# A two-layer MoE decoder trunk: f32r row broadcasts, low parts on VectorE, residual sum formed late, aligned ring of 38 weight pieces

## The chip, the cores and the metric

The kernel runs on one core of a Trainium2 chip. The metric is the device time of one execution in microseconds (us), as the median of several runs. A profile of one execution lies beside the runs.

## The reference

A sequence of 256 tokens of width 1024 goes through two layers. Each layer is a mixer (layer 0: a chunkwise mLSTM; layer 1: MoBA block-sparse attention) and a mixture of 16 experts (MoE). All is float32. Cut to what the change touches:

```python
shift, scale, gate = mods[layer, 0]          # from silu(c) @ w_ada + b_ada
y = mixer(modulate(x, shift, scale))
x = layer_norm(ALPHA * x + gate * y, ln_g[layer, 0], ln_b[layer, 0])
shift, scale, gate = mods[layer, 1]
h = modulate(x, shift, scale)
probs = softmax(h @ w_router)                # 16 experts in 4 groups
# best group by the sum of its top two (probs + b_router), then its top two experts
y = sum over the 2 experts of weight * (silu(h @ w_gate[e]) * (h @ w_up[e])) @ w_down[e]
x = layer_norm(ALPHA * x + gate * y, ln_g[layer, 1], ln_b[layer, 1])
```

The expert weights are 100.7 MB per layer and are all read, whatever the routing.

## The kernel before

**Weights.** All weights come in pieces of 512 KB (128 partitions x 1024 floats) that SyncE's queue (SP) issues in the order of the program. A piece goes into a slot of a ring and the slot is free when TensorE (PE) has used it. The ring has 20 slots (`RING * 2`), and around a MoE up to 17 more (`RING2`), so that 37 pieces can stand ready. By the addresses that the allocator gives in the built program, the 20 slots begin at multiples of 256 bytes within a partition and the 17 others 64 or 224 bytes past one.

**A MoE** uses 192 pieces: 8 blocks of two experts, each with a gate part, an up part and a down part of 8 pieces. The first block needs the routing; until then only prefetching can go on, and it stops when the ring is full.

**Routing chain, per layer.** The last mixer product `y(1,1)` on PE; VectorE (DVE) adds it to `xt` (L542, L543); PE transposes (`th`), ScalarE (ACT) copies to `xT`, PE forms `pr` and `pl`; DVE makes the logits `lg` (L993), ACT the exponentials `pexp`; DVE then walks through some 25 small operations (`s`, `ss` L1026, `pairs` L1036 to L1038, `el`, `gl`, `gn`, `en`) to `mask` (L1051). PE sums the mask into positions (`pp`), DVE makes `onehot` (L1075), PE gathers the chosen tokens into banks `ga` with products of `onehot` and the two float32r parts `xh` and `xl` of x, ACT and DVE modulate them into `xe` (L518, L520), and PE starts on the gate part (`pg`). All these wait for each other.

**Beside that chain.** `xl = x - xh` is made on GpSimd (POOL, L1003) in four pieces of 128x512. The residual sum `acc = ALPHA * (x * g + b)` is made on DVE in eight steps (L1295, L1296), from rows `lnps` that PE broadcasts from `rw` to all partitions (L497, sixteen float32 128x128 products per layer, each of which the trace records twice). The gate rows `adag` are broadcast the same way (L449, four float32 128x256 products per call, two calls per layer). In the MoE, `slots_T` transposes the one-hot matrix and sums the weights of the slots (`oT`, `wsl`, L1106 to L1118).

The order on each engine is that of a scheduler in the program which places instructions by their costs and what they wait for; `issue_after` holds one back until another is placed.

Of the kernel before, what the change touches and what calls it, by code (L numbers as in the profile page):

```python
# [18 lines left out]
P = 128  # L19
D = 1024  # L20
# [14 lines left out]
RING2 = 17  # L35
# [23 lines left out]
BIG = 1e30  # L59

def _columns(groups):

    at, span, o = {}, [], 0
    for g, names in enumerate(groups):
        o0 = o
        for n, w in names:
# [8 lines left out]
                             (("cb", KI), ("gn", KI), ("skip", KI), ("cw", 4 * KI), ("wif", KI * 8), ("bif", 2))))  # L75
CS, CS_SPAN, NCS = _columns(((("ident", P), ("sel4", 1), ("iota", SLOTS), ("selr", E)),
# [3 lines left out]
def constants():  # L80
# [16 lines left out]
    put("sel4", p % 32 == 0)  # L97
    m = np.zeros((P, 12))
# [50 lines left out]
def _body(ctx, tc, x, w_ada, a_w_in, a_wq, a_wk, a_wv, a_w_out, b_w_kv, b_wq, b_wo, moe_w_gate, moe_w_up,  # L149
# [6 lines left out]
    small = ctx.enter_context(tc.tile_pool(name="small", bufs=2))  # L156
    ring = ctx.enter_context(tc.tile_pool(name="ring", bufs=RING * 2))
# [13 lines left out]
    G.memset(rw, 0.0)  # L171
    nc.sync.dma_start(pk[0][:, 0:KD], pc[:, 0:KD])
# [158 lines left out]
    def ada_sum(j, hf, red, accs):  # L331

        ps = bankB(f"adaps{j}_{hf}")
        for z in range(2):
# [3 lines left out]
            if is_gate(j):  # L338
                for y in range(2):
                    r = 64 + 8 * (j // 3) + 4 * hf + 2 * z + y  # L340
                    T.matmul(o[:, P * y:P * y + P], ident[:, r:r + 32], rw, start=False, stop=(y == 1))
# [243 lines left out]
    wif = pe.tile([P, KI, 32], F32, name="wif")  # L585
    G.memset(wif, 0.0)
# [954 lines left out]
```

## Time and profile before

| | |
|---|---|
| median of 3 runs | 941.38 us (940.91 to 943.47) |
| the profiled execution's own time | 941.74 us |
| its span, first to last instruction | 940.0 us |
| mean granted TensorE clock | 0.986 of 2.4 GHz |
| PE busy | 905.2 us (96%) |
| DVE busy | 525.4 us (56%) |
| ACT, POOL busy | 336.0 us, 38.1 us |
| DMA | 318.56 MB, mean 339 GB/s |

The span has these stages: mixer A to about 310 us, routing of layer 0 to 332, MoE 0 to about 546, mixer B to 692, routing of layer 1 to 715, MoE 1 to about 922, and a tail to 940. A busy PE need not be the limit, since in a MoE its matmuls wait for pieces; the share of the DMA engines and the GB/s tell that apart.

### The profile page before, as it was taken

The page shows a single profiled execution, that of the slowest core. Times are in us where ns is not written, and L with a number is a line of the kernel's source. Part 1 is how long each engine was busy: PE and PEld are TensorE (multiplying, and loading weights), DVE is VectorE, ACT ScalarE, POOL GpSimd, SP SyncE. Part 2 cuts the span into 40 slices and gives each one's busy share as a digit, 9 for nine tenths or more (in the row PEclk, how much of TensorE's full clock was granted, in tenths as well). Part 3 has the DMA queues.
Part 4 walks back from the last instruction along what each step waited for, and adds up shares of the span by engine and source line. Part 5 has one row for each costly group of instructions (what it writes and reads, how often), then busy time and mean ns, then how long its engine had stood idle before and what let it go on. Part 6 is the DMA issues. An engine that isn't in the chain of part 4 may idle for free. (4 is left out here: it accounts for less than half of the span.)

```text
span 940.0 us, 14244 instructions
## 1 busy us (share of the span) xinstructions
PE 905.2 (96%) x5397; PEld 564.9 (60%) x5400; DVE 525.4 (56%) x992; ACT 336.0 (36%) x558; POOL 38.1 (4%) x48
## 2 busy tenths in 40 slices
PE   9999999999999899999999988999998999999995
PEld 5877988876777644334343478886764343434343
DVE  2476876867878823332333499898883223334317
ACT  3476666466564311111111054566542111101120
POOL 0010000000000200000000004021110000000000
PEclk9999999999999999999999998999998999999998
DMA  9999784787987979999999998877984999999992
GB/s 333 393 405 376 260 282 156 270 330 250 333 305 257 355 271 407 406 406 407 407 406 407 397 403 336 300 255 242 372 317 166 408 405 407 407 406 407 407 398 103
DMA packets 174253, 318.56 MB, mean 339 GB/s; under 512 B 10112, under 2 KB 28256, under 8 KB 174176
## 3 DMA queue, kind: packets, MB, share of 16 engines
q1 hardware_dynamic: 174032, 317.36, 91.2%
q8 instruction: 45, 0.74, 0.3%
q14 instruction: 32, 0.26, 0.1%
q10 hardware_dynamic: 144, 0.20, 0.1%
HBM read 316.47 MB, written 1.05 MB: 338 GB/s over the span
## 5 line engine op out<-in xcount | busy, mean ns | idle before, releaser
L1202 DVE SCALAR_TENSOR_TENSOR yl<-py,wsl,yh 128x512 fp32r<-128x512 f32 x28 | 21.0, 750 | 172.6 <-ACT yh L1201 172.6
L126 PE MATMUL pg<-w,xe 128*64 128x512 f32 x512 | 116.1, 596 | 0.0
L126 PE MATMUL pu<-w,xe 128*64 128x512 f32 x512 | 116.0, 596 | 0.0
L126 PE MATMUL py<-w,aT 128*64 128x512 f32 (+1 forms) x576 | 115.8, 547 | 0.2 <-DMA w<-in_moe_w_down_dram 0.2
L384 DVE SCALAR_TENSOR_TENSOR adacc<-ada,pk,adacc 128x512 f32<-128x512 f32 x112 | 87.3, 785 | 1.0
L126 PEld LDWEIGHTS py<-w,aT 128*64 128x64 f32 x576 | 40.9, 137 | 70.8 <-issue 61.2
L126 PEld LDWEIGHTS pu<-w,xe 128*64 128x64 f32 x512 | 35.7, 137 | 63.7 <-issue 61.4
L126 PEld LDWEIGHTS pg<-w,xe 128*64 128x64 f32 x512 | 34.8, 137 | 64.0 <-issue 58.9
L1168 ACT COPY aT<-aT 128x512 f32<-128x512 f32 x16 | 9.4, 585 | 141.0 <-PE aT L126 141.0
L542 DVE TENSOR_TENSOR lntmpe<-po,gate 128x512 f32<-128x512 f32 x56 | 36.1, 685 | 38.1 <-PE po L126 38.1
L1201 ACT ACTIVATE yh<-py,wsl 128x512 fp32r<-128x512 f32 x28 | 19.2, 687 | 81.1 <-PE py L126 81.1
L520 ACT ACTIVATE xe<-ga,coef 128x256 f32<-128x256 f32 x32 | 16.3, 561 | 76.6 <-PE ga L126 76.6
L262 PE MATMUL z<-hh,wz 128*128 128x256 f32 x128 | 37.6, 294 | 0.0
L543 DVE TENSOR_TENSOR acc<-acc,lntmpe 128x512 f32<-128x512 f32 x56 | 36.1, 684 | 0.0
L263 PE MATMUL z<-hl,wz 128*128 128x256 f32 x128 | 36.0, 281 | 0.0
L264 PE MATMUL z<-hh,wz 128*128 128x256 f32 x128 | 35.9, 280 | 0.0
L126 PE MATMUL ga<-onehot,xh 128*128 128x256 f32 x128 | 34.6, 305 | 0.0
L126 PE MATMUL ga<-onehot,xl 128*128 128x256 f32 x128 | 33.2, 296 | 0.0
L1161 DVE TENSOR_TENSOR a<-a,pu 128x512 f32<-128x512 f32 x16 | 11.0, 688 | 37.5 <-PE pu L126 18.5
L126 PEld LDWEIGHTS ga<-onehot,xh 128*128 128x128 f32 x128 | 26.2, 204 | 5.7 <-DVE acc L543 4.9
L126 PE MATMUL xm<-hh,win 128*128 128x256 f32 x144 | 28.8, 289 | 0.7 <-ACT hh L126 0.7
L1156 ACT ACTIVATE a<-pg 128x512 f32<-128x512 f32 x16 | 9.6, 597 | 53.2 <-PE pg L126 53.2
(384 smaller groups left out, 2024.8 us busy)
## 6 DMA issues: line engine op xcount, KB each, us to landing
w<-in_moe_w_gate_dram SPq DMA_DIRECT2D x128, 512.0 KB, 10.2
w<-in_moe_w_up_dram SPq DMA_DIRECT2D x128, 512.0 KB, 10.2
w<-in_moe_w_down_dram SPq DMA_DIRECT2D x128, 512.0 KB, 10.2
ada<-in_w_ada_dram SPq DMA_DIRECT2D x112, 512.0 KB, 6.9
win<-in_a_w_in_dram SPq DMA_DIRECT2D x16, 512.0 KB, 8.5
wz<-in_a_w_in_dram SPq DMA_DIRECT2D x16, 512.0 KB, 5.9
wout<-in_a_w_out_dram SPq DMA_DIRECT2D x16, 512.0 KB, 5.9
wv<-in_a_wv_dram SPq DMA_DIRECT2D x8, 512.0 KB, 6.1
```

The lines of the kernel that those rows point to most:

```text
L126: return self.tc.keep_in_program_order(f(*a, **kw))
L262: T.matmul(ps, l[0], r[0], start=start, stop=False, skip_group_check=True)
L263: T.matmul(ps, l[0], r[1], start=False, stop=False, skip_group_check=True)
L264: T.matmul(ps, l[1], r[0], start=False, stop=stop, skip_group_check=True)
L384: V.scalar_tensor_tensor(a, w[:, k, :], c, a, op0=OP.mult, op1=OP.add)
L520: A.activation(dst, ps, AF.Identity, bias=sh[:, k:k + 1], scale=sc[:, k:k + 1])
L542: V.tensor_tensor(tmp, y, gate[:, c], op=OP.mult)
L543: V.tensor_tensor(dst[:, t, c], dst[:, t, c], tmp, op=OP.add)
L1156: A.activation(a, pg, AF.Silu)
L1161: V.tensor_tensor(a, a, pu, op=OP.mult)
L1201: A.activation(yh, py, AF.Copy, scale=wsl[:, b:b + 1])
L1202: V.scalar_tensor_tensor(yl, py, wsl[:, b:b + 1], yh.bitcast(F32), op0=OP.mult, op1=OP.subtract)
```

## The change

1. **Float32r rows.** The rows of `lnps` and `adag` are split into a high and a low float32r part that stand in different partitions (`lnr`; `gp` from two DVE operations per call), and a 0/1 column `pick` adds both in one product: `lnps` is one 128x512 float32r product in place of four float32 ones of 128x128, `adag` two of 128x256 per bank in float32r.
2. **Low parts on DVE.** `xl` moves from POOL to DVE (`low_part`).
3. **Sum late, in x's place.** `acc` is `xt` itself, and its eight steps may only be placed after `onehot`.
4. **Gather.** For the first four experts all `xh` products come first, over four banks, then all `xl` products.
5. **Slots by one product.** `slots_T` is one float32r product of 128x160 per token tile with `wide` = identity, W high, W low. `wsl` is a sum over four columns.
6. **Ring.** `PAD` tiles put every slot at a multiple of 256 bytes; the ring gets one more piece, 38.
7. At the start `lnr` is loaded through one ring slot and split on POOL (a memset, two passes of 128x512 and a small copy); `wif` is read in place.

```diff
-RING2 = 17
+RING2 = 18
+PAD = 24, 48, 56
...
+    keep.tile([P, PAD[0]], F32, name="pad")
...
     def gate_rows(j):
         gt = keep.tile([P, D], F32, tag="gate", name=f"gate{j}")
+        parts = small.tile([P, 512], F32R, tag="lntmp", name=f"gp{j}")
+        hi, hl = parts[:, 0:256], parts[:, 256:512]
+        V.tensor_copy(hi, gaterow[j])
+        V.scalar_tensor_tensor(hl, hi.bitcast(F32), C("low"), gaterow[j], op0=OP.mult, op1=OP.add)
...
-                T.matmul(pg[:, 256 * g:256 * g + 256], ident[:, 32 * q:32 * q + 1].to_broadcast([P, P]), gaterow[j],
-                         start=True, stop=True)
+                T.matmul(pg[:, 256 * g:256 * g + 256], pick[:, 16 + q:17 + q].to_broadcast([P, P]), hl, start=True, stop=True)
...
-        for z in range(4):
-            r = 32 * q + 8 * ln + 4 * h + z
-            T.matmul(pg[:, P * z:P * z + P], ident[:, r:r + 1].to_broadcast([P, P]), rw, start=True, stop=True)
+        r = 8 * q + 2 * ln + h
+        T.matmul(pg, pick[:, r:r + 1].to_broadcast([P, P]), lnr, start=True, stop=True)
...
-            nc.sync.dma_start(rw[0:96, :], rows)
+            nc.sync.dma_start(rw[64:96, :], rows[64:96, :])
+            lnf = room("lnf", 1)[0][:, 0:512]
+            G.memset(lnf, 0.0)
+            for o in (0, 64):
+                nc.sync.dma_start(lnf[o:o + 16, :], rows[0:64, :].rearrange("(r z) n -> r (z n)", z=4))
+            G.tensor_copy(lnr, lnf)
+            G.tensor_tensor(lnr[64:P, :], lnf[64:P, :], lnr[64:P, :].bitcast(F32), op=OP.subtract)
+            G.tensor_copy(pick, C("pick"))
...
+            def low_part(t):
                 for h in range(2):
                     c = slice(512 * h, 512 * h + 512)
-                    G.tensor_tensor(xl[:, t, c], xt[:, t, c], xh[:, t, c].bitcast(F32), op=OP.subtract)
+                    V.tensor_tensor(xl[:, t, c], xt[:, t, c], xh[:, t, c].bitcast(F32), op=OP.subtract)
...
-            onehot(0)
+            low_part(0)
+            placed = onehot(0)
+            with tc.issue_after(placed):
+                low_part(1)
...
+            wide = sm("wide", [NT, P + 2 * E], F32R)
+            for t in range(NT):
+                V.tensor_copy(wide[:, t, 0:P], ident)
+            V.tensor_copy(wide[:, :, P:P + E], W)
+            V.tensor_tensor(wide[:, :, P + E:], W, wide[:, :, P:P + E].bitcast(F32), op=OP.subtract)
...
+                    banks = [bankB(f"ga{layer}_{q}_{k2}") for k2 in range(KD // 2)]
+                    for v in (xh, xl):
+                        for k2, ps in enumerate(banks):
+                            for n in range(4):
+                                product(ps, k2, n // 2, n % 2, v, start=(v is xh and n == 0), stop=(v is xl and n == 3), skip_group_check=True)
+                            if v is xl:
+                                out(k2, ps)
...
-                    T.transpose(pt[:, P * t:P * t + P], slots(t, 2 * b, 2).bitcast(F32), ident)
-                for t in range(NT):
-                    T.matmul(pt[:, 256:256 + E], slots(t, 2 * b, 2).bitcast(F32), W[:, t, :], start=(t == 0), stop=(t == NT - 1))
+                    T.matmul(pt[:, 160 * t:160 * t + 160], slots(t, 2 * b, 2), wide[:, t, :], start=True, stop=True)
...
-            acc = pm.tile([P, NT, D], F32, tag="acc", name=f"acc{layer}")
-            for h in range(2):
+            acc = xt
+            with tc.issue_after(placed):
+                for h in range(2):
```

**How the order moves.** DVE, layer 0, from the logits of the second half of the tokens to `pairs`, before:

```order
332 L993 SCALAR_TENSOR_TENSOR lg_3271<-pl_3267,lnrsm_3348,rb 128x16
333 L1295 SCALAR_TENSOR_TENSOR acc_3603<-xt,lnps_0_0_3372 128x512
334 L1017 TENSOR_REDUCE s_0_3363<-lg_3271 128x2
335 L1295 SCALAR_TENSOR_TENSOR acc_3603<-xt,lnps_0_1_3382 128x512
336 L1296 SCALAR_TENSOR_TENSOR acc_3603<-lnps_1_0_3377,acc_3603 128x512
337 L1024 RECIPROCAL s_0_3364<-s_0_3364 128x2
338 L1296 SCALAR_TENSOR_TENSOR acc_3603<-lnps_1_1_3387,acc_3603 128x512
339 L1026 SCALAR_TENSOR_TENSOR ss_3365<-pexp_3362,s_0_3364,pk 128x16 x2
340 L1295 SCALAR_TENSOR_TENSOR acc_3603<-xt,lnps_0_1_3382 128x512
341 L1036 TENSOR_TENSOR pairs_3404<-ss_3365 128x8x3
```

The same place on DVE after the change:

```order
336 L1014 SCALAR_TENSOR_TENSOR lg_3289<-pl_3285,lnrsm_3366,rb 128x16
337 L1040 TENSOR_REDUCE s_0_3379<-lg_3289 128x2
338 L1026 TENSOR_TENSOR xl_3288<-xt,xh_3287 128x512
339 L1047 RECIPROCAL s_0_3380<-s_0_3380 128x2
340 L1026 TENSOR_TENSOR xl_3288<-xt,xh_3287 128x512
341 L1049 SCALAR_TENSOR_TENSOR ss_3381<-pexp_3378,s_0_3380,pk 128x16 x2
342 L1059 TENSOR_TENSOR pairs_3409<-ss_3381 128x8x3
```

Five steps of the sum leave this place (and a sixth leaves the one between `gn` and `en`); two steps of `xl` come in.

DVE, layer 0, from the second `onehot` to the modulated tokens `xe`, after the change (before, only `mxi` and `W` stood between them):

```order
370 L1098 TENSOR_TENSOR onehot_0_3458<-pos_3448,cs 128x256
371 L1026 TENSOR_TENSOR xl_3288<-xt,xh_3287 128x512 x2
372 L1109 CAST mxi_3465<-mxc_3463 128x1
373 L1114 CAST wide_3467<-W_3450 128x2x16
374 L1117 SCALAR_TENSOR_TENSOR W_0_3472<-pos_3448,W_3450 128x32
375 L1344 SCALAR_TENSOR_TENSOR xt<-xt,lnps_0_0_3386 128x512
376 L1115 TENSOR_TENSOR wide_3467<-W_3450,wide_3467 128x2x16
377 L1344 SCALAR_TENSOR_TENSOR xt<-xt,lnps_0_0_3386 128x512
378 L1345 SCALAR_TENSOR_TENSOR xt<-lnps_1_0_3388,xt 128x512 x2
379 L534 TENSOR_SCALAR xe_0_3544<-ga_0_1_3546,coef 128x256 x2
380 L534 TENSOR_SCALAR xe_0_3544<-ga_0_3_3548,coef 128x256 x2
381 L1344 SCALAR_TENSOR_TENSOR xt<-xt,lnps_0_1_3390 128x512 x2
```

Two pieces of `xl` and four steps of the sum now stand ahead of `xe`, the other four behind it.

PE, layer 1, between the two products `pl` that give the logits, before:

```order
3069 L991 MATMUL pl_6697<-cs,lr_0_6729 128x16
3070 L983 MATMUL th_10_6752<-cs,xt 128x128 x4
3071 L983 MATMUL th_11_6758<-cs,xt 128x128 x4
3072 L497 MATMUL lnps_1_0_6807<-rw,cs 128x128 x3
3073 L497 MATMUL lnps_0_1_6812<-rw,cs 128x128 x4
3074 L988 MATMUL pr_1_6764<-xT_6698,wr 32x128 x4
3075 L497 MATMUL lnps_1_1_6817<-rw,cs 128x128
3076 L988 MATMUL pr_1_6764<-xT_6698,wr 32x128 x4
3077 L497 MATMUL lnps_1_1_6817<-rw,cs 128x128 x3
3078 L449 MATMUL adag_0_6823<-mr_5568,cs 128x256
3079 L991 MATMUL pl_6697<-cs,lr_1_6773 128x16
```

The same place on PE after the change:

```order
3034 L1012 MATMUL pl_6698<-cs,lr_0_6730 128x16
3035 L1004 MATMUL th_10_6753<-cs,xt 128x128 x4
3036 L1004 MATMUL th_11_6759<-cs,xt 128x128 x4
3037 L1009 MATMUL pr_1_6765<-xT_6699,wr 32x128 x4
3038 L467 MATMUL adag_0_6811<-gp_6808,pick 128x256 x2
3039 L1009 MATMUL pr_1_6765<-xT_6699,wr 32x128 x4
3040 L467 MATMUL adag_1_6815<-gp_6808,pick 128x256 x2
3041 L1012 MATMUL pl_6698<-cs,lr_1_6774 128x16
```

Eleven float32 row products and one of `adag` leave the stretch; all four `adag` products, now float32r, stand in it.

## Rows read from the trace of the kernel before

**Rows 1.** The page: GB/s of DMA in 40 equal slices of the span.

```profile
GB/s 333 393 405 376 260 282 156 270 330 250 333 305 257 355 271 407 406 406 407 407 406 407 397 403 336 300 255 242 372 317 166 408 405 407 407 406 407 407 398 103
```

**Rows 2.** Windows: busy time by engine, then granted clock, DMA share, GB/s.

```profile
284.00:310.00 26.00, 26.00 (x120) 18.87 (x120) 21.14 (x46) 10.98 (x19) 0.00 (x0) 1.00 0.78 273
304.00:316.00 12.00, 11.97 (x93) 8.76 (x92) 9.14 (x29) 4.54 (x9) 0.00 (x0) 1.00 1.05 390
328.00:330.00 2.00, 2.00 (x11) 2.00 (x11) 0.00 (x0) 0.91 (x2) 0.00 (x0) 0.50 0.02 4
...
340.00:540.00 200.00, 198.09 (x983) 83.84 (x982) 65.32 (x126) 26.16 (x44) 0.00 (x0) 1.00 1.05 405
541.00:545.00 4.00, 4.00 (x26) 2.50 (x24) 3.04 (x9) 0.00 (x0) 0.00 (x0) 1.00 1.05 408
566.00:592.00 26.00, 22.71 (x167) 21.61 (x166) 25.84 (x29) 10.91 (x21) 10.29 (x4) 0.87 0.90 333
672.00:692.00 20.00, 19.94 (x109) 14.43 (x108) 14.98 (x34) 6.61 (x12) 0.00 (x0) 1.00 0.96 357
```

**Rows 3.** Window inside the routing of layer 1, same columns.

```profile
704.00:706.00 2.00, 0.00 (x0) 0.00 (x0) 2.00 (x6) 0.00 (x0) 1.79 (x2) 0.86 0.05 19
```

**Rows 4.** Timeline: SP's first issue after the full ring, layers 0 and 1.

```profile
334.25 2.08 SPq L212 DMA_DIRECT2D w<-in_moe_w_up_dram  x3
...
716.55 0.37 SPq L212 DMA_DIRECT2D w<-in_moe_w_up_dram  x1
```

**Rows 5.** Timeline of the gate rows at the end of mixer A (start, duration).

```profile
297.08 1.99 PE L449 MATMUL adag<-mr,cs 128*128 128x256 f32 x8
```

**Rows 6.** Timeline of the routing of layer 0: start, duration, engine, line.

```profile
317.63 0.23 DVE L993 SCALAR_TENSOR_TENSOR lg<-pl,lnrsm,rb 128x16 f32<-128x16 f32 x1
...
318.11 4.95 POOL L1003 TENSOR_TENSOR xl<-xt,xh 128x512 fp32r<-128x512 f32 x4 [165.61 <-ACT xh L1000]
...
320.32 1.55 DVE L1026 SCALAR_TENSOR_TENSOR ss<-pexp,s,pk 128x16 f32<-128x16 f32 x2
...
325.44 0.19 DVE L1051 SCALAR_TENSOR_TENSOR mask<-gn,en 128x32 bf16<-128x32 f32 x1
...
326.82 0.42 DVE L1075 TENSOR_TENSOR onehot<-pos,cs 128x256 fp32r<-128x256 f32 x1
326.95 0.55 PE L126 MATMUL ga<-onehot,xh 128*128 128x256 f32 x1
...
331.00 0.28 PE L126 MATMUL ga<-onehot,xh 128*128 128x256 f32 x1
331.12 0.28 PE L126 MATMUL ga<-onehot,xl 128*128 128x256 f32 x1
...
332.29 7.09 PE L126 MATMUL pg<-w,xe 128*64 128x512 f32 x32
```

**Rows 7.** Timeline of the routing of layer 1.

```profile
699.07 0.29 DVE L990 COPY lr<-pr 128x128 f32<-128x128 f32 x1
...
700.14 0.29 PE L991 MATMUL pl<-cs,lr 128*128 128x16 f32 x2
...
702.82 0.38 DVE L1026 SCALAR_TENSOR_TENSOR ss<-pexp,s,pk 128x16 f32<-128x16 f32 x2
...
703.27 2.52 POOL L1003 TENSOR_TENSOR xl<-xt,xh 128x512 fp32r<-128x512 f32 x2 [1.56 <-ACT xh L1000]
703.34 1.25 DVE L1037 TENSOR_TENSOR pairs<-ss 128x16 f32<-128x16 f32 x1
704.50 0.16 DVE L1038 TENSOR_TENSOR pairs<-ss 128x8 f32<-128x8 f32 x1
704.59 1.27 DVE L1031 TENSOR_TENSOR el<-ss 128x24 f32<-128x24 f32 x1
...
707.35 0.19 DVE L1051 SCALAR_TENSOR_TENSOR mask<-gn,en 128x32 bf16<-128x32 f32 x1
```

**Rows 8.** The tile view of acc: durations min/median/max in ns.

```profile
L1295 DVE SCALAR_TENSOR_TENSOR acc<-xt,lnps x8: 627/678/680, 314.2 to 701.3; 128x512 f32<-128x512 f32 x8
```

More of the change, by code (lines that the diff above doesn't have):

```diff
@@ L97, in constants @@
     put("sel4", p % 32 == 0)
+    m = np.zeros((P, 20))
+    for r in range(16):
+        m[r, r] = m[64 + r, r] = 1
+    for q in range(4):
+        m[32 * q, 16 + q] = m[32 * q + 16, 16 + q] = 1
+    put("pick", m)
+    put("low", -((p % 32) // 16))
     m = np.zeros((P, 12))
@@ L1092, in gather, with product, out @@
                 xe = pm.tile([P, KD, 256], F32, tag="xe", name=f"xe{layer}_{q}")
+                def product(ps, k2, kk, t, v, **kw):
+                    k = 2 * k2 + kk
+                    T.matmul(ps[:, 256 * kk:256 * kk + 256], v[:, t, P * k:P * k + P], slots(t, 4 * q, 4), **kw)
+                def out(k2, ps):
+                    for kk in range(2):
+                        k = 2 * k2 + kk
+                        affine(xe[:, k, :], ps[:, 256 * kk:256 * kk + 256], sc, sh, k, k2 % 2)
+                if q == 0:
+                    banks = [bankB(f"ga{layer}_{q}_{k2}") for k2 in range(KD // 2)]
[5 more added lines that the diff above has]
+                                out(k2, ps)
+                    return xe
                 for k2 in range(KD // 2):
@@ L1095, in gather @@
                     for kk in range(2):
-                        k = 2 * k2 + kk
-                        n = 0
-                        for t in range(NT):
-                            for v in (xh, xl):
-                                T.matmul(ps[:, 256 * kk:256 * kk + 256], v[:, t, P * k:P * k + P], slots(t, 4 * q, 4),
-                                         start=(n == 0), stop=(n == 3))
-                                n += 1
-                    for kk in range(2):
-                        k = 2 * k2 + kk
-                        affine(xe[:, k, :], ps[:, 256 * kk:256 * kk + 256], sc, sh, k, k2 % 2)
+                        for n in range(4):
+                            product(ps, k2, kk, n // 2, (xh, xl)[n % 2], start=(n == 0), stop=(n == 3))
+                    out(k2, ps)
                 return xe
@@ L1240, in overflow @@
                             pt = bankB(f"oxT{layer}_{t}{h}")
+                            xs = small.tile([P, 512], F32, tag="lntmp", name=f"ox{layer}_{t}{h}")
+                            c = slice(512 * h, 512 * h + 512)
+                            V.tensor_tensor(xs, xh[:, t, c].bitcast(F32), xl[:, t, c].bitcast(F32), op=OP.add)
                             for k in range(4):
-                                T.transpose(pt[:, P * k:P * k + P], xt[:, t, 512 * h + P * k:512 * h + P * k + P], ident)
+                                T.transpose(pt[:, P * k:P * k + P], xs[:, P * k:P * k + P], ident)
                             for k in range(4):
@@ L1289, in moe @@
             slots_T(0)
[L1290 to L1296 removed]
+            acc = xt
+            with tc.issue_after(placed):
+                for h in range(2):
+                    c = slice(512 * h, 512 * h + 512)
+                    pg, pb_ = rows_[2 * h:2 * h + 2]
+                    for t in range(NT):
+                        V.scalar_tensor_tensor(acc[:, t, c], xt[:, t, c], ALPHA, pg, op0=OP.mult, op1=OP.mult)
+                        V.scalar_tensor_tensor(acc[:, t, c], pb_, ALPHA, acc[:, t, c], op0=OP.mult, op1=OP.add)
             def rest():
```

32 lines of the change are left out of this document (15 added, 17 removed).

## The prediction

> **What bounds the kernel now.** I read GB/s by slice first, to see where DMA is the limit. Slices 15 to 22 and 31 to 38 run at 397 to 408 GB/s [rows 1]: these are the two MoEs. The windows confirm it: from 340 to 540 us the DMA share is 1.05 at 405 GB/s, while PE looks 99% busy only because its matmuls wait for pieces [rows 2]. One gate part takes PE 7.09 us [rows 6], and its 8 pieces of 0.524 MB take DMA 8 x 0.524 MB / 405 GB/s = 8 x 1.29 = 10.4 us. So a MoE ends when its last piece has landed, and faster PE or DVE work inside it buys nothing.
>
> What can move a MoE's end is when its loading starts again. In layer 0 the window from 328 to 330 moves 4 GB/s [rows 2]: the 37 slots are full. SP issues the next piece at 334.25 [rows 4], about 2 us after `pg` starts at 332.29 [rows 6] and frees its first slots. In layer 1 the rate is down to 19 GB/s between 704 and 706 [rows 3] and the next issue is at 716.55 [rows 4]. **Every us by which `pg` starts earlier is a us off the kernel**, until the stall is used up; it is about 6 us long in layer 0 (328.3 to 334.25) and 10 us in layer 1.
>
> Before each routing PE is the limit: 26.00 of 26 us busy from 284 to 310 at a DMA share of 0.78, and 19.94 of 20 from 672 to 692 [rows 2]. Between them, in the first part of mixer B, DVE is: 25.84 of 26 us [rows 2].
>
> **The change part by part** (clock at 2.4 GHz unless said).
>
> *Gate rows ahead of the routing.* `adag` takes PE 1.99 us [rows 5] in a stretch where PE is the limit, in each layer. The four float32r products of the same width that replace it are like the gather's, which start 0.12 us apart [rows 6]: 0.5 us. Gain 1.5 us per layer; nothing if PE then waits for the two new DVE operations that form `gp`, which stand only a few places ahead. I take **-1.5 and -1.5** (0 to -2 each).
>
> *Layer 0, logits to mask.* Before: 317.63 to 325.63, 8.0 us [rows 6]. Six steps of the sum stand inside at 0.68 us each [rows 8], and `ss` takes 1.55 us while POOL is in `xl`, against 0.38 us in layer 1 where POOL is idle [rows 6, 7]. After: lg and s 0.3; then the exponentials on ACT, covered by one `xl` of 0.68 (I use the row of the sum, same shape, on the same engine [rows 8]); reciprocal and a second `xl` 0.8; `ss` 0.4; and from `pairs` to `mask` what layer 1 takes without contention. That is 703.34 to 707.54 less the two operations stretched by POOL, 1.25 and 1.27 where a neighbour takes 0.16 [rows 7]: 4.2 - 2.2 = 2.0, and 0.1 for the first. The waits between engines add 0.4. Together 4.8 us, so -3.2. Against it: `lnrsm` of the second token half now stands on ACT behind the two copies to `xT`, which moves the logits by what I put at +0.6 (0 to +1.0). Net **-2.6** (-1.5 to -3.2).
>
> *Layer 1, logits to mask.* The contention of POOL and DVE goes: -2.2 [rows 7]. The second `pl` at 700.14 waited for `lnps` and `adag` on PE although `lr` was done at 699.36 [rows 7]: -0.8. Two steps of the sum leave this chain and two `xl` come in, at equal price [rows 8]. DVE now takes the two additions of the second token half before the first half's logits, and both gate activations of ACT stand ahead of the exponentials: +1.0 (0 to +1.5). Net **-2.0** (-1 to -3).
>
> *Mask to `pg`.* From the second `onehot` (ends 327.24) to `pg` 5.05 us, of which the gather on PE is 32 products from 326.95 to 332.29, the first part at half clock (granted 0.50 between 328 and 330) and the rest 0.12 us apart [rows 2, 6]. DVE now does two `xl`, four steps of the sum and four small operations there before `xe`: 6 x 0.68 + 4 x 0.16 = 4.7 us. The second `xl` is ready 1.4 us after `onehot`, and the gather asks for it after its 16 `xh` products, 1.9 us or later: hidden. `xe` of the second bank starts at 4.7 instead of 3.25 us, but `pg` takes its eight k-steps 7.09 / 8 = 0.89 us apart and wants it at its third, 1.8 us after it starts: hidden too, by `pg` itself. Without that cover it would cost up to 1.5 us. **0** per layer, from -1.3 (all at full clock: 32 x 0.12 = 3.8 us) to +1.7 (all at half: 6.8 us).
>
> *One more piece.* When the stall begins one more piece stands in the ring, and DMA is idle anyway: **-1.29 us per layer, -2.6**, if the stall outlasts its loading. In layer 0 the stall of 6 us loses 4.1 to the earlier `pg` and 1.3 to this piece, so it just does.
>
> *Alignment.* All pieces are aligned now. In the MoE the mix of before moves 405 GB/s, and a stretch (541 to 545) of aligned pieces alone 408 [rows 2]. That is 0.7% of the roughly 200 us of one MoE, 1.4 us, if all of it were alignment; the smaller requests that run along in the MoE explain some, so I take **-0.5 per layer, -1.0**. The prefetch from 304 to 316, mostly in unaligned slots, runs at 390 [rows 2], 4% less, but it ends in the stall, which hides it.
>
> The Trainium skill, "DMA: Bandwidth & Descriptors", section "How a descriptor splits into AXI transactions", says that a descriptor that starts off a 256-byte boundary costs extra beats for bytes that it doesn't use. The 390 against 408 GB/s agrees with it; the 405 in the MoE does not show it. By that rule alone the sum would gain about 3.5 us more per layer, as the second rival works out from rows.
>
> *The rest.* `lnps` at the start of mixer B saves PE about 3 us, but DVE is the limit there [rows 2] and gets 0.7 us more of `gp`: **-0.5** (0 to -2.8). `slots_T` is inside the DMA-bound MoE: 0. The start has two more small transfers, a memset and a few POOL passes: **+0.3** (0 to +1). The tail's broadcasts are done before its chain begins: 0.
>
> Sum: -3.0 - 2.6 - 2.0 + 0 - 2.6 - 1.0 - 0.5 + 0.3 = **-11.4 us**. The profiled execution's own time is 941.74, so 930.3; it stands 0.36 above the median of the runs, which by the same sum goes to 930.0. I round towards the smaller gain, since most of the terms rest on waits that could reappear: **930.5 us**.
>
> **The rivals.**
>
> *A. The gain is partly given back inside routing.* What leaves the chain comes back as waits on DVE, which carries 12 steps of 0.68 us per layer in new places, POOL's four `xl` among them. For it: DVE is the engine of the whole chain, and a late low part or a late `xe` delays `pg` one to one. Against it: the two covers worked out above. Half of the routing and gate row gains (7.6) lost: 934.5; all but the piece, the alignment and the gate rows lost: 935 to 936.
>
> *B. Alignment pays in the whole MoE.* If unaligned pieces cost 408 / 390 - 1 = 4.6% there too, 17 of 37 slots make 2.1% of the roughly 200 us of loading per MoE: 4.2 us, against the 0.5 I took: 2 x 3.7 more, **923 us**. Against it: 405 GB/s in the mix [rows 2]. It is what the rule of the Trainium skill, "DMA: Bandwidth & Descriptors", section "How a descriptor splits into AXI transactions", would do here.
>
> *C. Slower: PE stays at half clock.* The float32 row products kept PE busy during routing; without them it idles more. If the clock of 0.50 [rows 2], which in the rows ends within the gather, lasted through the gather, `pg` and the following up part in both layers, the gather costs +1.7, and the first two parts take 28.4 instead of 14.2 us, against loading that needs from the first freed slot 2 + 15 x 1.29 = 21.3 us: +7.1. Together +8.8 per layer, 930.5 + 17.6 = **948 us**. It decides from about +5.8 per layer, a half clock until just past the end of `pg`. Against it: PE's load from the gather on is what it was, and there the clock came back within it.
>
> *D. The loading hides everything.* If the MoE's end did not depend on when `pg` starts, only mixer terms would remain: 938 to 940. Against it: the dead stretches of [rows 2, 3].
>
> **How the numbers follow.** My forecast (927 to 933.5) 0.58; A 0.20 (933.5 to 938); B 0.12 (920 to 927); D 0.06, half of it within 0.3%; C 0.04. 0.3% of 941.4 is 2.8 us, about what a measurement of this kernel can tell from no change. Faster takes all of the forecast, A and B and a little of D: 0.91; same 0.05; slower 0.04. The range leaves out C, D and the far half of B: **924 to 937.5**.
>
> **What would show it.** Right: from the logits of the second half to the end of `mask` about 4.8 us in layer 0; no small DVE operation over 1 us in layer 1; the first issue after the stall 4 us earlier in layer 0 (330.2) and some 10 us earlier in layer 1 (706.8: 4.1 + 1.3 + 0.5 + 0.5 + 3.5, less 0.3 of the start); MoE stretches at 405 to 408 GB/s with equal length less one piece. Wrong: `xe` or the low part as what ends PE's wait in the gather; 0.50 clock in the first `pg`; GB/s above 412 in the MoE (B); SP waiting for POOL at the start.

## The result, and the profile after

The changed kernel takes 929.48 us (median of 4 runs, 927.69 to 929.63) against 941.48: a ratio of 0.9864, interval 0.9846 to 0.9883, so faster by 1.2 to 1.5%. The forecast was 930.5 us. The sum was right to a microsecond, but not all of its terms were: three of them were off by 1.6 to 3.5 us, in both directions, and the experiments below are mostly about these.

The profiled execution took 929.63 us with a span of 927.9. The two traces can be cut at the same events. The landings are those of SP's weight pieces; "logits" means the start of `lg`, "restart" the first piece to land after the full ring, and the end is that of the span. Forecasts are the terms of the prediction, put to the stage in which each would show.

| stage | before | after | moved | forecast |
|---|---|---|---|---|
| start to the first `y` product | 214.55 | 216.41 | +1.86 | +0.3 |
| to the second logits, layer 0 | 103.08 | 101.69 | -1.39 | -0.9 |
| to the end of `mask` | 8.00 | 4.44 | -3.56 | -3.2 |
| to the restart | 12.66 | 12.88 | +0.22 | 0 |
| to the last landing of MoE 0 | 201.13 | 202.21 | +1.08 | -1.8 |
| to the second logits, layer 1 (mixer B) | 161.04 | 156.28 | -4.76 | -1.8 |
| to the end of `mask` | 7.07 | 4.46 | -2.61 | -2.2 |
| to the restart | 12.50 | 12.55 | +0.05 | 0 |
| to the last landing of MoE 1 | 202.23 | 200.42 | -1.81 | -1.8 |
| to the end | 17.74 | 16.59 | -1.15 | 0 |

The page of the kernel after, GB/s in 40 slices, answers to [rows 1]:

```profile
GB/s 331 383 377 405 225 306 181 212 399 209 352 299 213 393 339 406 407 407 406 407 407 407 383 403 370 340 225 225 374 322 254 404 407 407 407 407 407 407 399 124
```

Both MoEs run at 399 to 407 GB/s, as before, but for slice 22 (510 to 533 us), which falls to 383. Windows of the kernel after (columns as in [rows 2]), around the gather of layer 0, at the start, and inside both MoEs:

```profile
322.00:327.00 5.00, 4.41 (x22) 3.49 (x22) 4.84 (x21) 0.00 (x0) 0.00 (x0) 0.50 1.05 408
40.00:60.00 20.00, 18.32 (x165) 16.45 (x164) 12.42 (x19) 10.24 (x16) 5.72 (x6) 1.00 1.00 360
340.00:520.00 180.00, 178.61 (x862) 72.73 (x857) 56.02 (x107) 24.71 (x41) 0.00 (x0) 1.00 1.05 406
720.00:900.00 180.00, 178.57 (x860) 73.30 (x856) 55.33 (x103) 25.87 (x44) 0.00 (x0) 1.00 1.05 406
```

The first line shows PE at half clock through the first part of the gather. By the trace's records of the clock it lasts from 321.0 to 327.8 us; in the kernel before it lasted from 326.6 to 330.0. The longer half clock can't be put down to the change: in e1, whose routing is the same, it ends at 324.6, 3.4 us after it began. Windows of e1 and of the kernel after:

```profile
325.00:328.00 3.00, 3.00 (x23) 2.29 (x24) 2.65 (x7) 2.29 (x5) 0.00 (x0) 1.00 1.01 388
...
325.00:328.00 3.00, 3.00 (x17) 3.00 (x16) 3.00 (x9) 0.00 (x0) 0.00 (x0) 0.53 1.05 406
```

From `mask` to the restart e1 takes 12.28 us and the kernel after 12.88, so that stage varies by 0.6 us with the same routing. The second line above shows that DMA moves 360 GB/s between 40 and 60 us, where the same window of the kernel before moved 405:

```profile
40.00:60.00 20.00, 18.91 (x169) 17.08 (x168) 11.65 (x20) 10.77 (x17) 3.53 (x4) 1.00 1.06 405
```

The timeline of the kernel after in the routing of layer 0 answers to [rows 6]:

```profile
318.10 0.23 DVE L1014 SCALAR_TENSOR_TENSOR lg<-pl,lnrsm,rb 128x16 f32<-128x16 f32 x1 [0.34 <-PE pl L1012]
...
318.64 0.69 DVE L1026 TENSOR_TENSOR xl<-xt,xh 128x512 fp32r<-128x512 f32 x1
...
319.39 0.67 DVE L1026 TENSOR_TENSOR xl<-xt,xh 128x512 fp32r<-128x512 f32 x1
319.98 0.38 DVE L1049 SCALAR_TENSOR_TENSOR ss<-pexp,s,pk 128x16 f32<-128x16 f32 x2
...
322.35 0.19 DVE L1074 SCALAR_TENSOR_TENSOR mask<-gn,en 128x32 bf16<-128x32 f32 x1
...
324.03 3.96 PE L135 MATMUL ga<-onehot,xh 128*128 128x256 f32 x16
...
327.80 2.09 PE L135 MATMUL ga<-onehot,xl 128*128 128x256 f32 x16
...
329.82 1.51 PE L135 MATMUL pg<-w,xe 128*64 128x512 f32 x6
```

`ss` takes 0.38 instead of 1.55 us. The 16 `xh` products take 3.96 us at half clock, the 16 `xl` products 2.09 at full, and `pg` follows the last product of the gather: DVE's `xe` is not what it waits for. In layer 1, as in [rows 7]:

```profile
693.91 0.23 DVE L1014 SCALAR_TENSOR_TENSOR lg<-pl,lnrsm,rb 128x16 f32<-128x16 f32 x1 [0.49 <-PE pl L1012]
...
696.32 0.17 DVE L1060 TENSOR_TENSOR pairs<-ss 128x16 f32<-128x16 f32 x1
...
698.18 0.19 DVE L1074 SCALAR_TENSOR_TENSOR mask<-gn,en 128x32 bf16<-128x32 f32 x1
```

The operation on `pairs` that took 1.25 us beside POOL takes 0.17.

SP's first issue after the full ring, layers 0 and 1, answers to [rows 4]:

```profile
331.78 0.88 SPq L226 DMA_DIRECT2D w<-in_moe_w_up_dram  x2
...
707.37 0.88 SPq L226 DMA_DIRECT2D w<-in_moe_w_up_dram  x2
```

It is 2.5 us earlier in layer 0 (forecast 4) and 9.2 us earlier in layer 1 (forecast 10); the start, 1.9 us late, is in both. In all the kernels here, in both layers, it comes 1.96 us after `pg` starts.

### The profile page after: what moved, and what is told of

Read it like the earlier page. It is cut to its first block, busy times and chain, and to the rows that moved or that the text cites. A ratio compares the mean times of both kernels' runs of the same rounds, so it can differ in the third digit from the quotient of the medians.

```text
span 927.9 us, 13867 instructions
## 1 busy us (share of the span) xinstructions
PE 887.9 (96%) x5205; PEld 542.0 (58%) x5208; DVE 529.0 (57%) x1016; ACT 334.9 (36%) x558; POOL 30.4 (3%) x42
## 4 chain that ended last, share of the span: by engine, by line
PE 37%; DMA 10%; DVE 6%; issue 1%; ACT 1%; DVEq 0%; ACTq 0%; SPq 0%
PE pg L135 8%; PE py L135 7%; PE pu L135 7%; DMA w<-in_moe_w_up_dram 4%; PE ga L135 3%; PE po L135 3%; DMA w<-in_moe_w_down_dram 2%; DVE adacc L398 1%; DMA w<-in_moe_w_gate_dram 1%; PE bo L1482 1%; DMA wq<-in_b_wq_dram 1%; DMA ada<-in_w_ada_dram 1%; PE by L276 1%; PE bv L276 1%; PE by L278 1%
## 5 line engine op out<-in xcount | busy, mean ns | idle before, releaser
L135 PE MATMUL pu<-w,xe 128*64 128x512 f32 x512 | 118.5, 596 | 0.2 <-DMA w<-in_moe_w_up_dram 0.2
L559 DVE TENSOR_TENSOR xt<-xt,lntmpe 128x512 f32<-128x512 f32 x56 | 36.0, 681 | 0.0
L135 PE MATMUL ga<-onehot,xh 128*128 128x256 f32 x128 | 31.6, 324 | 0.2
L135 PE MATMUL ga<-onehot,xl 128*128 128x256 f32 x128 | 27.4, 280 | 0.0
```

The costliest lines, as they stand in the source:

```text
L135: return self.tc.keep_in_program_order(f(*a, **kw))
L559: V.tensor_tensor(dst[:, t, c], dst[:, t, c], tmp, op=OP.add)
```

## The experiments

Each kernel is the kernel after with one edit unless said. The medians are of four to ten runs. The kernel before was run beside each group of kernels and had medians of 941.3 to 943.4; ratios are to that one. The scatter of one kernel's runs is 1 to 5 us, so differences of 1 to 2 us are read from the stages of the traces and not from the medians.

**e1: the load of `lnr` later.** The six lines that load and split `lnr` move in front of `gM, gcol = gates_part()`:

```diff
     def start_loads(q):
...
-            lnf = room("lnf", 1)[0][:, 0:512]
-            G.memset(lnf, 0.0)
...
+    lnf = room("lnf", 1)[0][:, 0:512]
+    G.memset(lnf, 0.0)
...
     gM, gcol = gates_part()
```

> The kernel after, with the load and split of lnr moved from about 42 us to the end of the gates part of mixer A (about 150 us). Theory: at 42 to 53 us six small transfers in a row fill SP's window of loads in flight, so that DMA runs dry and PE gets its first y product 1.9 us later than before; moved to where DMA is not the limit, the first y comes at 214.5 us again and the kernel at 927.0 to 928.0 us (1.5 to 2.4 us less than 929.5). Rival: the two us are absorbed later in mixer A by PE waiting for something else, and the time stays within 0.5 us of the kernel after.

Measured: 926.79 us (925.89 to 927.41), ratio 0.9841 (0.9825 to 0.9857). The first `y` product starts at 214.15 us. Its window shows the start mended:

```profile
40.00:60.00 20.00, 18.89 (x170) 17.07 (x169) 11.70 (x20) 10.84 (x17) 3.44 (x4) 1.00 1.06 405
```

SP's own timeline shows the cause, first in the kernel before, then in the kernel after:

```profile
41.94 1.66 SPq L212 DMA_DIRECT2D wv<-in_a_wv_dram  x2
...
40.59 0.34 SPq L676 DMA_DIRECT2D rw<-in_rows_dram  x1
41.95 1.54 SPq L680 DMA_DIRECT2D lnf<-in_rows_dram  x2
44.52 1.69 SPq L226 DMA_DIRECT2D wv<-in_a_wv_dram  x2
```

Where a free slot is not what it waits for, SP issues its next transfer just when the one eight places ahead has landed: the first of `lnf` at 41.95, and the transfer eight places ahead lands at 41.88; `wv` at 44.52, and that one lands at 44.45. Each small transfer takes such a place until it lands. Four in a row (`pk`, two of `cs`, `rw`) stood in both kernels and were covered by the pieces in flight; with the two of `lnf` the first `wv` piece is issued at 44.52 instead of 41.94, and DMA falls to 360 GB/s. The theory holds (the time is 0.2 us under its range), the rival falls.

**e2: PE kept busy before `pp`.**

```diff
-WARM = 5, 4
+WARM = 20, 4
```

> The kernel after, with 20 instead of 5 warming products on PE between the last logits and pp in each layer (they work on constants, and the result is not used). Theory: the granted clock is 0.50 for 6.8 us in the routing of layer 0 and 3.4 us in layer 1 because PE idles 3.4 us before pp; kept busy, it stays at 1.0, the gather takes about 4 us instead of 5.8, and pg starts 1.5 to 2 us earlier in each layer: 926 to 927 us. Rival: DVE, which has two low parts and four steps of the sum ahead of xe, becomes the limit of pg: under 1 us in all. Second rival: the warming products reach past the mask and delay pp: 0 to +1 us.

Measured: 929.51 us (929.04 to 930.34), no gain. The timeline of this kernel shows why, layer 0 first:

```profile
318.38 4.53 PE L333 MATMUL warmp<-onesq 128*128 128x512 bf16 x19
...
322.82 0.19 DVE L1074 SCALAR_TENSOR_TENSOR mask<-gn,en 128x32 bf16<-128x32 f32 x1
...
324.32 2.40 PE L135 MATMUL ga<-onehot,xh 128*128 128x256 f32 x16
...
694.76 5.77 PE L333 MATMUL warmp<-onesq 128*128 128x512 bf16 x18 [0.22 <-issue]
...
698.41 0.19 DVE L1074 SCALAR_TENSOR_TENSOR mask<-gn,en 128x32 bf16<-128x32 f32 x1
...
700.38 0.17 PE L1080 MATMUL pp<-mask,before 128*128 128x16 bf16 x1
```

In layer 0 the clock stays at 1.0, the `xh` part of the gather takes 2.40 instead of 3.96 us, and the restart comes 11.09 us after `mask` instead of 12.88 (12.28 in e1): the theory. In layer 1 the clock had already fallen when the warming products began:

```profile
691.50:698.00 6.50, 6.28 (x31) 3.10 (x25) 3.91 (x26) 4.05 (x9) 0.00 (x0) 0.50 1.05 406
```

The products last until 700.5, until 698.2 at half clock, and `pp` comes 1.8 us after `mask`: the second rival. The rest went in stages that the edit does not touch: mixer B took 0.9 us more, the loading of MoE 0 0.7 (202.9 us), the start 0.5. Work put into a gap to hold the clock must still fit into it when the clock is low.

**e3: 37 pieces.**

```diff
-RING2 = 18
+RING2 = 17
```

> The kernel after with 37 instead of 38 pieces in the ring, all aligned. Theory: each layer loads one piece more after its routing, 1.29 us: 932.0 us (+2.6). Rival: in layer 0 the 38th piece landed at 331.6, after pg had begun at 329.8, so that it saved little there: +1.3 us, from layer 1 alone.

Measured: 930.20 us (928.99 to 931.37), ratio 0.9878 (0.9862 to 0.9895), +0.7. From restart to last landing layer 1 takes 201.80 us instead of 200.42, one piece more. Layer 0 takes 201.77 instead of 202.21, which looks like the rival. But the edit changed another thing there: ACT issues the constants for mixer B at 531.14 us,

```profile
531.14 0.38 ACTq L202 DMA_DIRECT2D group<-in_cst_dram  x1
```

and not at 507.90 as in the kernel after, where SP waits 5.1 us for them (see e8). So the two can't be compared in layer 0. Without that wait, kernels with 37 pieces take 201.77 (e3), 201.13 (before), 201.16 (e10) and 200.50 us (e12) from restart to last landing there, and those with 38 take 200.20 and 200.17 (e8, e11): about 1 us. And the rival's reason does not hold: in the kernel after the 38th piece lands at 331.56, after `pg` has begun but before SP's first issue into a freed slot (331.78); in e3, with 37, the piece of that number lands at 335.28. So the extra piece pays in both layers; the +0.7 in the time hides it, since e3 is spared the wait.

**e4, e10, e12: the low parts and the sum apart.** e4 puts `xl` back on POOL in the kernel after. e10 is the kernel before with only the sum held behind `onehot`, e12 the kernel before with only `xl` on DVE.

```diff
 e4
-                    V.tensor_tensor(xl[:, t, c], xt[:, t, c], xh[:, t, c].bitcast(F32), op=OP.subtract)
+                    G.tensor_tensor(xl[:, t, c], xt[:, t, c], xh[:, t, c].bitcast(F32), op=OP.subtract)
 e10, on the kernel before
...
+            placed = onehot(0)
...
-            for h in range(2):
...
+            with tc.issue_after(placed):
+                for h in range(2):
...
 e12, on the kernel before
-                    G.tensor_tensor(xl[:, t, c], xt[:, t, c], xh[:, t, c].bitcast(F32), op=OP.subtract)
+                    V.tensor_tensor(xl[:, t, c], xt[:, t, c], xh[:, t, c].bitcast(F32), op=OP.subtract)
```

e4: 

> The kernel after with the low parts xl back on POOL. Theory: POOL and DVE hinder each other again, and small DVE operations of the mask chain take over 1 us where they run beside xl (2 to 4 of them per layer), against two xl of 0.68 us that leave DVE's chain: +1 to +3 us. Rival: the chain on DVE is the limit and 1.4 us less work on it per layer pays: -1 to -2 us.

e10: 

> The kernel before with one part of the change alone: the steps of the sum may only be placed after onehot (acc stays a tile of its own). Theory: six steps of 0.68 us leave the mask chain of layer 0 and one or two that of layer 1, POOL's xl still stretches ss, so lg to mask takes 8.0 - 3.0 = 5 us in layer 0 and 6.4 in layer 1, pg starts earlier by the same: 937.5 to 938.5 against 941.5. Rival: POOL's xl reaches further into the chain now that it runs earlier, and takes half of it back: 939.5 to 940.5.

e12: 

> The kernel before with another part of the change alone: xl on DVE, the sum left where it was. Theory: the two parts pay only together, since each makes room for the other in the same chain. Here the four low parts of 0.68 us come into the chain beside the six steps of the sum: from the second logits to mask 9.3 us in layer 0 (before 8.0), about 7.5 in layer 1 (before 7.1), though no small operation is stretched any more: 942.5 to 943.5 us. Rival: the end of the contention of POOL and DVE is what pays, whatever else stands in the chain: lg to mask 5 to 6 us in both layers, 938 us.

Second logits to the end of `mask`, layer 0 and layer 1, and the time:

| | sum early | sum late |
|---|---|---|
| `xl` on POOL | before: 8.00, 7.07 us; 941.48 | e10: 7.28, 6.13; 938.47 (ratio 0.9968, 0.9954 to 0.9981); e4: 7.44, 6.40; 934.02 (0.9922, 0.9905 to 0.9938) |
| `xl` on DVE | e12: 8.88, 7.01; 941.22 (0.9991, 0.9977 to 1.0006) | after: 4.44, 4.46; 929.48 |

Timeline of e4, layer 0:

```profile
318.84 4.93 POOL L1026 TENSOR_TENSOR xl<-xt,xh 128x512 fp32r<-128x512 f32 x4 [164.26 <-ACT xh L1021]
...
319.66 1.70 DVE L1049 SCALAR_TENSOR_TENSOR ss<-pexp,s,pk 128x16 f32<-128x16 f32 x2
321.39 1.20 DVE L1059 TENSOR_TENSOR pairs<-ss 128x24 f32<-128x24 f32 x1
322.51 1.29 DVE L1060 TENSOR_TENSOR pairs<-ss 128x16 f32<-128x16 f32 x1
323.72 0.16 DVE L1061 TENSOR_TENSOR pairs<-ss 128x8 f32<-128x8 f32 x1
```

And of e10:

```profile
318.04 4.96 POOL L1003 TENSOR_TENSOR xl<-xt,xh 128x512 fp32r<-128x512 f32 x4 [165.56 <-DVE s L1017]
...
318.97 1.59 DVE L1026 SCALAR_TENSOR_TENSOR ss<-pexp,s,pk 128x16 f32<-128x16 f32 x2
320.60 1.20 DVE L1036 TENSOR_TENSOR pairs<-ss 128x24 f32<-128x24 f32 x1
321.71 0.17 DVE L1037 TENSOR_TENSOR pairs<-ss 128x16 f32<-128x16 f32 x1
321.80 1.23 DVE L1038 TENSOR_TENSOR pairs<-ss 128x8 f32<-128x8 f32 x1
```

As long as POOL works on `xl`, three small operations of the chain take 1.2 to 1.3 us each, in e4 and in e10, and each of them ends 0.03 to 0.04 us after one of POOL's pieces (1.26 to 1.29 us each) ends; one that starts between two pieces takes 0.17. In the kernel before, steps of the sum stood in that time and a single `ss` was held in layer 0, so taking the steps out alone (e10) lets more of the small operations run into POOL. In e12 the chain on DVE holds both the sum and `xl`:

```profile
318.35 0.68 DVE L1295 SCALAR_TENSOR_TENSOR acc<-xt,lnps 128x512 f32<-128x512 f32 x1
318.94 1.28 DVE L1003 TENSOR_TENSOR xl<-xt,xh 128x512 fp32r<-128x512 f32 x2
320.25 0.68 DVE L1296 SCALAR_TENSOR_TENSOR acc<-lnps,acc 128x512 f32<-128x512 f32 x1
```

In the chain the sum held late gains 0.72 and 0.94 us by itself, `xl` on DVE loses 0.88 and gains 0.06, and both together gain 3.56 and 2.61. In the whole time each alone gains 0 to 3 us, but with the sum late, `xl` on DVE is worth 4.5 us (e4). That is more than e4's +1 to +3, and in its direction. e12's theory held for the chain in layer 0 (8.88 for 9.3); for the whole time its 942.5 to 943.5 was not met, and neither was the rival's 938. e10's time is that of its theory (937.5 to 938.5), but its chain is not: layer 0 gave 0.7 of 3.0 us, by the rival's mechanism, and 1.6 us of the gain stand in mixer B (159.47 against 161.04; e12 has 162.44 there), where the edit has no part.

**e5: `lnps` in float32 again.** The matmuls of `ln_bank` are those of the kernel before, from `rw`; the load of `lnr` is left out with them.

```diff
-        r = 8 * q + 2 * ln + h
-        T.matmul(pg, pick[:, r:r + 1].to_broadcast([P, P]), lnr, start=True, stop=True)
+        for z in range(4):
+            r = 32 * q + 8 * ln + 4 * h + z
+            T.matmul(pg[:, P * z:P * z + P], ident[:, r:r + 1].to_broadcast([P, P]), rw, start=True, stop=True)
```

> The kernel after with the lnps rows again as four float32 products of 128x128 from rw (adag stays float32r, and the load of lnr at 42 us is gone). Theory: in mixer B, which the kernel after goes through in 148.1 us from the last landing of MoE 0 to the last y product (before 152.9), these products are on the path although DVE looks full: mixer B 151 us (+3), and the missing load gives 2 us back at the start: 930 to 931 us. Rival, as the prediction had it: DVE is the limit there, mixer B stays at 148.1 to 148.6 us, and the time falls to 927.5 us by the start alone.

Measured: 931.27 us (930.57 to 932.62), ratio 0.9884 (0.9853 to 0.9915). From the last landing of MoE 0 to the second logits it takes 160.23 us (before 161.04, after 156.28): the theory, at +4, of which 3.5 stand ahead of the last `y` product (151.64 against 148.12). All kernels with float32r rows take 155.3 to 157.4 us for this stage, those with float32 rows 159.5 to 162.4. The rival, which was the prediction's own step, falls. The first `y` product is back at 214.27 us, as in e1. The tile views of `lnps`, e5:

```profile
L514 PE MATMUL lnps<-rw,cs x96: 270/275/376, 309.5 to 693.7; 128*128 128x128 f32 x96
```

and after:

```profile
L513 PE MATMUL lnps<-lnr,pick x12: 388/481/502, 311.6 to 687.2; 128*128 128x512 f32 x12
```

A row of 512 is one record in place of eight. In mixer B the copies of the rows to `lnrow` on ACT end 33.8 us after the last landing of MoE 0 in the kernel before, 34.2 in e5 and 30.9 after; the last `bk` product ends at 49.4, 49.3 and 44.0 us. By these marks the rows stood in a chain from PE by ACT to x of that layer, and `bk` came behind it; that this chain is the whole of the 4 us is argued, not tested. DVE was as full as the prediction said, before and after:

```profile
543.00:593.00 50.00, 43.38 (x313) 40.45 (x312) 49.24 (x72) 26.76 (x47) 10.29 (x4) 0.90 0.97 366
...
542.00:592.00 50.00, 43.66 (x330) 40.72 (x328) 49.50 (x72) 28.70 (x49) 10.72 (x4) 0.97 0.97 359
```

But the costliest group in that time, in the kernel before, is not work of this part of the mixer:

```profile
L384 DVE SCALAR_TENSOR_TENSOR adacc<-ada,pk,adacc 128x512 f32<-128x512 f32 x19 | 18.3, 968 | 0.1
```

`adacc` sums up the modulation vectors for later stages, and the program puts it as filler between other work. 18 of the 49 busy us are such work.

**e6: `adag` in float32 again.** DVE's two operations that split `gaterow` are left out with it.

```diff
-                T.matmul(pg[:, 256 * g:256 * g + 256], pick[:, 16 + q:17 + q].to_broadcast([P, P]), hl, start=True, stop=True)
+                T.matmul(pg[:, 256 * g:256 * g + 256], ident[:, 32 * q:32 * q + 1].to_broadcast([P, P]), gaterow[j], start=True, stop=True)
```

> The kernel after with the adag rows again as float32 products from one part (gp is not formed). Theory: PE is the limit ahead of each routing, and the four products cost 2.0 us instead of 0.5: the last y products come 1.5 us later in layer 0 and 1.5 us more in layer 1; inside the routing adag stands ahead of the second pl or behind it, 0 to +1 us each: 932.5 to 934 us. Rival: PE has slack there or gp on DVE costs as much: within 0.8 us of 929.5.

Measured: 929.58 us (929.11 to 930.73), ratio 0.9866 (0.9835 to 0.9896). The time is the rival's. First `y` to second logits, layer 0: 103.35 us against 101.69 after and 103.08 before, +1.66: the theory. Layer 1: last landing to second logits 156.12 against 156.28: the rival; the last `y` product does come 1.2 us later, but the logits don't. The 1.66 us of layer 0 went again between `mask` and the restart (11.83 against 12.88, with the half clock over at 327.5 in this execution, 3.4 us long) and in the loading of MoE 0 (201.09 against 202.21; the kernels with the constants in the same place as the kernel after take 201.1 to 202.9 there).

**e7, e9: alignment.** e7 leaves out the padding tiles, e9 moves the 18 slots beside the ring of 20 by 64 bytes, to 192 bytes past a multiple of 256 in the built program.

```diff
 e7
-    keep.tile([P, PAD[0]], F32, name="pad")
-    ctx.enter_context(tc.tile_pool(name="edge", bufs=1, side="right")).tile([P, PAD[2]], F32, name="padr")
...
-            pm.tile([P, PAD[1]], F32, name=f"pad{layer}")
 e9
-PAD = 24, 48, 56
+PAD = 24, 32, 56
```

e7: 

> The kernel after without the padding tiles, so that the 18 slots beside the ring of 20 begin off a multiple of 256 bytes again; the order on all engines is the same. Theory: mixed with aligned pieces they cost nothing that can be seen, since the pieces of a MoE land 1.285 us apart before and 1.284 after: within 0.8 us of 929.5, and slower only in runs of unaligned pieces alone. Rival, the rule on unaligned descriptors: 18 of 38 pieces 4.6% longer, +4 us in each MoE: 937 us.

e9: 

> The kernel after with the 18 slots beside the ring of 20 moved 64 bytes off a multiple of 256 (the ring stays on multiples); the order on all engines is the same. Theory, after e7 in which all 38 slots stood off a multiple and the pieces of a MoE landed 1.36 us apart: what unaligned pieces cost is hidden as long as aligned ones lie between them, since the loads in flight share a limit of 1.285 us a piece, as in the kernel before: within 1 us of 929.5, pieces 1.285 to 1.29 us apart on the mean. Rival: each unaligned piece costs its 0.07 us: 18 of 38 of 384 pieces, +9 to +13 us, 939 to 942.

e7 took 949.99 us (948.36 to 951.21), ratio 1.0082 (1.0050 to 1.0115), slower than the kernel before; e9 930.84 (929.67 to 932.02), ratio 0.9885 (0.9862 to 0.9908). The expectation for e7 was wrong in its edit: by the built program, without the padding not 18 but all 38 slots begin off a multiple of 256 bytes, at 160 or 224. A window in MoE 0 of e7:

```profile
345.00:525.00 180.00, 177.06 (x826) 71.73 (x824) 53.95 (x101) 24.13 (x40) 0.00 (x0) 1.00 1.05 387
```

and of e9:

```profile
340.00:520.00 180.00, 178.29 (x858) 73.18 (x860) 56.02 (x107) 24.71 (x41) 0.00 (x0) 1.00 1.05 406
```

With all slots unaligned 0.524 MB take 1.355 us at 387 GB/s; aligned, 1.291 at 406; with 18 of 38 unaligned, 406 as well. In e9 an unaligned piece lands 1.31 us after an aligned one, and an aligned one 1.26 us after an unaligned one (medians; 1.28 from piece to piece in the kernel after): together they take what aligned pieces alone take. So the loss of 5% is real, and it is hidden where aligned and unaligned pieces alternate, as they do in e9 and in the kernel before. e9's time is 1.3 us above 929.5, a little outside its theory's 1 us and far from the rival's 939.

**e8, e11: the best versions.** e8 is e1 with the constants of mixer B loaded by SP behind the weights of MoE 0; e11 is e8 with `adag` in float32 in the routing of layer 1.

```diff
 e8
-    load_group(pb, cs, CS_SPAN, cst, 2)
-    dist = C("dist")
...
         k_part(0)
+    load_group(pb, cs, CS_SPAN, cst, 2, nc.sync)
+    dist = C("dist")
...
 e11
...
-            gate = gate_rows(jm + 2)
+            gate = gate_rows(jm + 2, layer == 0)
```

e8: 

> The kernel of e1 (load of lnr late), and the constants group for mixer B issued on SP behind MoE 0's pieces instead of on ACT at 508 us, where it stands in the queues behind 8 pieces and SP waits 5.1 us for it, as only eight transfers are in flight at a time. Theory: without that wait MoE 0 loads 1.5 to 2 us faster (199.7 instead of 201.5 us from the first landing after the routing to the last): 924.8 to 925.5 us against e1's 926.8. Rival: the wait is made up by PE's backlog or by the later start of mixer B's own loads: within 0.5 us of 926.8.

e11: 

> The kernel of e8 with adag in float32 again in the routing of layer 1 only. Theory, from e6, where the last y to the second logits took 6.8 us in layer 1 against 8.2 with gp: the two DVE operations that form gp stand in the chain there, and without them layer 1 gets 1.2 to 1.4 us back: 924.7 us. Rival: the 1.4 us of e6 came from another order of that run, or the float32 products on PE delay pl by as much: within 0.5 us of 926.

In the kernel after, ACT issues these constants at 507.90 us, in the timeline

```profile
507.90 0.38 ACTq L202 DMA_DIRECT2D group<-in_cst_dram  x1
```

and the waits of SP between 490 and 530 us show (what it waited for: us in total, times, longest)

```profile
SPq L226 <- DMA group<-in_cst_dram: 5.1, 1, 5.1
```

In the kernel before ACT issued them at 543.2, behind the last piece of MoE 0. Why the scheduler moved them is not shown. In e8 this wait is gone and MoE 0 loads in 200.20 us instead of e1's 201.45 and after's 202.21; the time is 926.05 (924.57 to 927.95), ratio 0.9819 (0.9788 to 0.9850). The stage shows the theory, but the medians can't tell e8 from e1. e11 took 925.32 us (924.08 to 928.71), ratio 0.9835 (0.9812 to 0.9858). Its last landing to second logits is 156.20 us, the same as after: the theory of `gp` in the chain falls, and e11 is e8 within the scatter. Its last `y` product ends 147.2 us after the last landing, 0.9 earlier than after, and the logits don't follow, as in e6. e1, e8 and e11 take 925 to 927 us, below the kernel after by 3 to 4 us.

Two parts of the change were not undone by themselves: the order of the gather (4) and the one product of `slots_T` (5). What they are worth is open.

## Why the prediction was right, and where it was not

**Right in mechanism and size.** What bounds the kernel: both MoEs stay at 406 GB/s, and in every kernel SP's first issue follows the start of `pg` by 1.96 us. Layer 0, logits to `mask`: 4.8 us forecast, 4.44 measured. Layer 1: contention 2.2, measured 2.61 for that stretch. The extra piece: 1.29 us per layer forecast; 1.4 in layer 1 (e3) and about 1 in layer 0 (e3 and others against e8). There the stall "just does" outlast the loading, as the prediction has it, by 0.2 us (331.56 against 331.78). `mask` to the restart: 0 forecast, +0.22 and +0.05 measured, less than the 0.6 us between the kernel after and e1, whose half clock is shorter. DVE's new work there is hidden, as forecast: `pg` starts with the end of the gather and runs in 7.09 us as before. Rival A (given back inside routing) and C (half clock through `pg`) did not happen: the clock is back to 1.0 before `pg`.

**Right in layer 0 alone.** The gate rows: 1.5 us forecast per layer, 1.66 in layer 0 (e6), nothing in layer 1. The step "Before each routing PE is the limit" failed there: in e6 the last `y` product of layer 1 comes 1.2 us later and the logits don't; in e11 it comes 0.9 us earlier and they don't either. What the logits wait for instead was not found.

**Wrong, too small.** The step "`lnps` at the start of mixer B saves PE about 3 us, but DVE is the limit there": forecast -0.5 (0 to -2.8), measured 4 us by e5. DVE is 98 to 99% busy in the first 50 us of mixer B before and after, and the stage became shorter all the same. The rows stood on a chain through PE and ACT, and more than a third of DVE's busy time was filler for later stages, which the busy share does not tell apart.

**Wrong, too large.** Alignment, forecast -0.5 per layer: 0 against the kernel before, since 405 GB/s with 17 of 37 slots unaligned is what aligned slots give (406 in the kernel after and in e9). The 408 that the prediction took for aligned pieces, in a stretch of 4 us, was not seen in a MoE. Rival B did not decide here. But e7 shows a loss of the size that it worked out from rows, 387 against 406 GB/s (406 / 387 - 1 = 4.9%; the rival had 4.6%), once no piece is aligned, and the change with the padding is 20 us faster than without it. Rival B is tied to the Trainium skill, "DMA: Bandwidth & Descriptors", section "How a descriptor splits into AXI transactions", which tells of bytes that a descriptor fetches below its start. In these runs it is the written side, the slot, that moves off the boundary, so e7 agrees in direction and does not show that mechanism.

**Not foreseen.** The start, +0.3 forecast, cost 1.9 us (e1 gives 2.3 back): the bound of +1 had looked at the two transfers as small and at POOL's passes, not at their places among the eight in flight. The loading of MoE 0 lost about 2 us to the constants of mixer B on ACT's queue (e8 and e11 take 200.2 us, the kernels with the constants in that place 201.1 to 202.9); the prediction had no term for it. And the end after the last landing is 1.15 us shorter. All kernels made from the kernel after have this, e4, e5 and e6 too (15.4 to 16.9 us), and e10 and e12 don't (17.5), so `xl`, the rows or the gate rows alone do not explain it; its cause stays open.

Two sums of the prediction are slightly off and moved nothing: half of 7.6 us lost gives 934.3 and not 934.5, and the terms of layer 1 put the issue at 706.95 and not 706.8.

That the total came out within 1 us is luck in part. By stages, mixer B missed by 3.0 us to one side (3.5 more from the rows, less the 1.5 of the gate rows; the rest is within what that stage scatters), the end by 1.1 and the three stages of the routings by 1.3 together; the start missed by 1.6 and MoE 0 by 2.9 to the other.

## What to carry to other kernels

Two engines that hinder each other in a chain, with filler work between, must be taken apart together: here taking the contention alone gained 0 us, and the same edit gained 4.5 once the filler was out. Where a queue has a fixed number of transfers in flight, count small transfers as places, and don't put several in a row where DMA is the limit. A busy share near 100% does not make an engine the limit: look for how much of it is filler and for what the next stage waits for, before an edit elsewhere is costed at nothing. And before two kernels are compared for one edit, check that nothing else moved: in e3 a transfer on another queue did, and hid what the edit cost in one layer.

## What the runs showed of the hardware

- Pieces of 512 KB in slots off a multiple of 256 bytes take 5% longer (1.355 against 1.291 us, e7 and the kernel after) when all slots are off, and nothing that can be seen (406 GB/s) when they alternate with aligned ones (e9).
- A DVE operation of 0.17 us that starts beside a POOL operation on two SBUF tensors takes 1.20 to 1.30 us and ends within 0.1 us after POOL's piece of 1.26 us does (e4, e10 and the kernel before): it seems to be held until that piece ends.
- A transfer of 32 KB in SP's stream takes one of eight places until it lands. Two of them, behind four other small ones, delayed PE's first `y` product by 1.9 to 2.3 us (kernel after against before and e1).
- In the routing of layer 0 the granted clock was 0.50 from 321.0 to 327.8 us in the kernel after and from 321.2 to 324.6 in e1, with the same work on PE. Both times PE was idle for 3.4 us ahead of `pp`, and the clock fell within that time (kernel after) or 0.9 us behind it (e1); with PE kept busy there (e2) it stayed at 1.00. From `mask` to the restart they took 12.88, 12.28 and 11.09 us.
